# One layer of hybrid attention: a half's second x group is split in the middle of the second projection tile, and in the output stages both loads stand at the beginning

## The chip, the core and the metric

The kernel runs on one core of a Trainium2 chip. The metric is the device time of one launch in microseconds (us); lower is better. The core has five engines that work through their own instruction streams, each in order: TensorE (PE in the rows, with PEld for its weight loads), VectorE (DVE), ScalarE (ACT), GpSimd (POOL) and SyncE (SP), which issues all of this kernel's transfers.

## What is computed

One decoder layer over 2048 tokens of width 1024. RMSNorm, one combined input projection, two attention mixers with eight heads each, gates, one output projection and the residual:

```python
hdn = rmsnorm(x, norm_gain[i])
proj = jnp.einsum("bsd,de->bse", hdn, w_in[i])
q_a, k_a, v_a, g_a, q_b, k_b, v_b, g_b = jnp.split(proj, split_at, axis=-1)
...
o_a, _, _ = banded_attention(q_a, k_a, v_a, A_WINDOW - 1, sinks=sinks_a[i])
o_a = o_a.reshape(b, S, A_WIDTH).astype(x.dtype) * jax.nn.silu(g_a)
...
o_b = dilated_attention(q_b, k_b, v_b)
o_b = o_b.reshape(b, S, B_WIDTH).astype(x.dtype) * jax.nn.silu(g_b)
mixed = jnp.concatenate([o_a, o_b], axis=-1)
x = x + jnp.einsum("bse,ed->bsd", mixed, w_out[i])
```

Mixer A is a causal window of 128 tokens with learned sinks. Mixer B attends under three patterns (window, dilation) and merges them by their softmax denominators. All of it is float32.

## The kernel before, in words

**Stages, blocks, halves.** Eight stages run one after the other: four of kind B (two heads of mixer B each), two of kind A (four heads of mixer A each), two of kind O (512 output columns each). A stage goes over four blocks of 512 tokens, and a block over two halves of 256 tokens; that makes 64 halves. In a B or A stage a half has two projection tiles (`tt` 0 and 1, 128 tokens each, eight chunks `c` of the 1024 input columns) and then one (B) or two (A) gate tiles of eight chunks. In an O stage a half has two output tiles.

**x in two parts.** A float32 product is made of three matmuls over a high and a low part of each operand (`mm3`, L244 in the rows). So a half needs its x, or in the O stages its mixed input, as xh and xl. `x_load` brings half of it (512 KB, four chunks, tile `xs`, two buffers); a half has two such loads, 0 and 1. `x_split` makes two chunks of it: a copy on ScalarE to xh (L155) and a subtraction to xl (L157), on GpSimd for groups 0 and 1 and for the last two halves of a stage, on VectorE otherwise. A half has four such groups; 0 and 1 read load 0, 2 and 3 read load 1. xh and xl have six buffers each, so group 2 of the next half takes the buffer of this half's group 0. In the first stage ScalarE also squares the next half's x (`squares`, L189), VectorE and a matmul with a column of ones sum it up (L198), and GpSimd raises it to a power: rst, the row factor of the norm (L182). rst is then transposed on TensorE (L211) into RB.

**Leaving PSUM.** When a projection tile is done, ScalarE squares its q and k part (sq, L409) and copies its v part with rst as scale (V, L410); VectorE then makes the rotary products (L419, L421) and the rest of V (L310). With that the tile's PSUM buffer (pj, two of them) is free for the tile after next.

**What sets the order.** `proj` is a generator that yields after every chunk; between the yields a driver puts in the pieces of attention that are due (scores, transposes, products with V, merging). The order so written is not yet the program's: the framework's scheduler takes the instructions of all engines with their dependencies and its own estimate of their times, and lays down each engine's stream. It can put an instruction far ahead of its place in the code when its inputs and buffers are free. Each engine, and the SP queue, then keeps to that stream.

The places that the change touches are in `proj` (B and A stages) and `proj_out` (O stages), where the next half `nx` is prepared. At the program's beginning `late_constants` also fills the zero rows of two tiles klz on GpSimd (L90).

Of the kernel before, what the change touches and what calls it, by code (L numbers as in the profile page):

```python
# [28 lines left out]
def f32(ap):  # L29
    return ap.bitcast(F32)  # L30
# [3 lines left out]
def hybrid_layer(ctx, tc, xT, xn, x, wB, wA, wO, ng, gains, sinks, rot, masks, ident, out):  # L34
# [116 lines left out]
    def x_split(si, hf, g):  # L151
        f = XS[si, hf, g // 2][:, 2 * (g % 2):2 * (g % 2) + 2]
        h = xp.tile([128, 2, 256], F32R, name="xh", bufs=XB)
        l = xp.tile([128, 2, 256], F32R, name="xl", bufs=XB)
        nc.scalar.activation(h, f, AF.Copy)  # L155
        eng = nc.gpsimd if g < 2 or hf >= 6 else nc.vector
        eng.tensor_tensor(l, f, f32(h), op=OP.subtract)  # L157
        XG[si, hf, g] = (h, l)
# [87 lines left out]
    def proj(si, sb):  # L246
# [22 lines left out]
        for half in range(2):  # L269
            hf = 2 * sb + half  # L270
            nx = next_half(si, hf)
# [6 lines left out]
            for tt in range(2):  # L278
# [3 lines left out]
                for c in range(KC):  # L282
                    xh, xl = xg[c // 2]
                    s = slice(tt * 128, tt * 128 + 128)
                    mm3(pj, (xh[:, c % 2, s], xl[:, c % 2, s]), wq[c], c, c == 0, c == KC - 1)
                    if last and half == 1 and tt == 1:
                        W[si + 1][2](c)
                    yield 490
                if tt == 0 and nx:
                    x_load(*nx, 1)  # L290
                    x_split(*nx, 0)
                    x_split(*nx, 1)
                    if si == hf == 0:
                        late_constants(1)
                        rb_make(0)
                    rope_tables(*nx)
                    if si == 0 and hf < 7:
                        for g in range(2):
                            squares(XS[nx + (g,)], g)
                    rb_load(*nx)  # L300
# [214 lines left out]
    def proj_out(si, sb, wq, wg, last):  # L515
# [4 lines left out]
        for half in range(2):  # L520
            hf = 2 * sb + half
            nx = next_half(si, hf)
            xg = [XG.pop((si, hf, g)) for g in range(4)]
            if nx:
                x_load(*nx, 0)
            for tt in range(2):
                r = 2 * half + tt
                orow = bass.AP(tensor=out.tensor, offset=out.offset + (512 * sb + r) * DM + idx * 512, ap=[[4 * DM, 128], [1, 512]])
# [4 lines left out]
                for n in range(2 * KC):  # L533
# [7 lines left out]
                    if last and half == 1 and tt == 1:  # L541
                        W[si + 1][2](c)
                        W[si + 1][3](c)
                    if nx and tt == 1 and c in (1, 3):
                        x_split(*nx, 2 + c // 2)
                    yield 650
                while deferred:
                    yield from deferred.pop(0)()
                if tt == 0 and nx:
                    x_load(*nx, 1)  # L550
                    x_split(*nx, 0)
                    x_split(*nx, 1)
                res_load()
                if tail:
                    for o in range(2):
# [484 lines left out]
```

## Time and profile before

| | us |
|---|---|
| three runs | 1264.9, 1262.76, 1270.4 (median 1264.9) |
| the profiled execution | 1271.72 |
| its span, first to last instruction | 1269.9 |
| TensorE busy | 1179.8 (93%) |
| VectorE, ScalarE, GpSimd busy | 867.5, 837.1, 685.3 |
| mean granted TensorE clock | 0.970 of 2.4 GHz |

In the rows further down each instruction is named by line, engine, operation and out<-in tiles, without buffer numbers; "[2.27 <-POOL xl L157]" says that its engine stood idle for 2.27 us before it and what ended that. A matmul's length in the rows covers its pipeline, so neighbours overlap. The granted clock is 1.0 or 0.5, which is 2.4 or 1.2 GHz.

### The profile page before, as it was taken

Reading aid. Unit: us, or ns where it says so; the run is one execution under the profiler, and the core shown is the slowest. Engines: PE = TensorE matmul, PEld = TensorE weight load, DVE = VectorE, ACT = ScalarE, POOL = GpSimd, SP = SyncE. Lnnn points to the kernel's source line nnn. Section 1 sums busy time; section 2 is a strip of 40 time slices with the busy share of each in tenths; the row PEclk is TensorE's granted clock in tenths of the full one; section 3 lists DMA queues with packets and bytes.
Section 4 is the critical chain, followed back from the end, with each engine's and each line's share of the span. In section 5 each row is a group of like instructions: output and inputs, shape, how many; then the busy total and the mean of one; then the engine's idle time right before and its main releaser. Section 6 shows DMA issues by size and latency. Waiting matters only on the chain. (4 is left out here: it accounts for less than half of the span.)

```text
span 1269.9 us, 25442 instructions
## 1 busy us (share of the span) xinstructions
PE 1179.8 (93%) x8328; PEld 1143.5 (90%) x8328; DVE 867.5 (68%) x2288; ACT 837.1 (66%) x2418; POOL 685.3 (54%) x788
## 2 busy tenths in 40 slices
PE   6898979988799898898998999999899999999899
PEld 6798979988699898898997999998799998999898
DVE  5666678776667677776877879888777868622221
ACT  6567777777668587676877767786776877513221
POOL 4876644566454755545676566673556565333122
PEclk9899989999999899898998999999899999999999
DMA  7454678776677776787866775555223235566551
GB/s 215 128 148 114 176 214 243 211 202 185 193 212 232 198 198 181 219 235 197 221 200 191 212 199 150 149 165 165 91 73 109 80 97 157 164 197 205 177 188 70
DMA packets 196883, 220.98 MB, mean 174 GB/s; under 512 B 34312, under 2 KB 143632, under 8 KB 196752
## 3 DMA queue, kind: packets, MB, share of 16 engines
q1 hardware_dynamic: 196752, 219.37, 59.2%
q8 instruction: 66, 1.08, 0.4%
q14 instruction: 65, 0.53, 0.1%
HBM read 164.44 MB, written 54.86 MB: 173 GB/s over the span
## 5 line engine op out<-in xcount | busy, mean ns | idle before, releaser
L244 PE MATMUL pj<-wh,xh 128*128 128x384 f32 (+1 forms) x1008 | 334.1, 334 | 18.6 <-ACT xh L155 6.7
L244 PE MATMUL pj<-wl,xh 128*128 128x384 f32 (+1 forms) x1008 | 334.9, 332 | 1.4 <-DVE wl L102 0.8
L244 PE MATMUL pj<-wh,xl 128*128 128x384 f32 (+1 forms) x1008 | 331.9, 331 | 1.1 <-POOL xl L157 0.8
L157 POOL TENSOR_TENSOR xl<-xs,xh 128x512 fp32r<-128x512 f32 x158 | 213.7, 1365 | 143.8 <-ACT xh L155 139.1
L155 ACT ACTIVATE xh<-xs 128x512 fp32r<-128x512 f32 x252 | 153.5, 627 | 115.8 <-PE pj L244 98.8
L244 PEld LDWEIGHTS pj<-wh,xh 128*128 128x128 f32 x1008 | 194.4, 193 | 22.4 <-ACT xh L155 7.1
L244 PEld LDWEIGHTS pj<-wl,xh 128*128 128x128 f32 x1008 | 194.6, 193 | 3.6 <-DVE wl L102 1.1
L244 PEld LDWEIGHTS pj<-wh,xl 128*128 128x128 f32 x1008 | 194.4, 193 | 3.5 <-DVE xl L157 1.3
L574 DVE TENSOR_TENSOR ptl<-pt,pth 128x512 fp32r<-128x512 f32 (+3 forms) x232 | 141.6, 619 | 42.2 <-ACT pth L573 40.2
L244 PE MATMUL pj<-xh,wgh 128*128 128x256 f32 x496 | 147.1, 297 | 10.7 <-DVE V L310 8.4
L244 PE MATMUL pj<-xh,wgl 128*128 128x256 f32 x496 | 145.3, 293 | 0.0
L244 PE MATMUL pj<-xl,wgh 128*128 128x256 f32 x496 | 144.7, 292 | 0.0
L573 ACT ACTIVATE pth<-pt 128x512 fp32r<-128x512 f32 (+3 forms) x232 | 123.1, 543 | 25.6 <-PE po L645 9.4
L430 POOL TENSOR_TENSOR t<-t,t 128x256 f32<-128x256 f32 (+1 forms) x96 | 79.2, 826 | 80.9 <-DVE t L421 57.2
L244 PEld LDWEIGHTS pj<-xh,wgh 128*128 128x128 f32 x496 | 97.7, 197 | 12.9 <-DVE V L310 5.8
L446 DVE TENSOR_TENSOR t<-t,fac 128x256 f32<-128x256 f32 (+1 forms) x96 | 76.9, 815 | 33.0 <-POOL fac L182 30.1
L244 PEld LDWEIGHTS pj<-xh,wgl 128*128 128x128 f32 x496 | 97.7, 197 | 0.8
L814 ACT ACTIVATE P<-P,scD 128x128 f32<-128x128 f32 (+3 forms) x128 | 71.6, 560 | 40.5 <-DVE scD L813 39.6
L244 PEld LDWEIGHTS pj<-xl,wgh 128*128 128x128 f32 x496 | 97.8, 197 | 0.4
L157 DVE TENSOR_TENSOR xl<-xs,xh 128x512 fp32r<-128x512 f32 x94 | 79.8, 859 | 20.2 <-ACT xh L155 19.8
L182 POOL TENSOR_TENSOR fac<-un,mhalf 128x8 f32<-128x8 f32 (+1 forms) x48 | 85.3, 1778 | 2.7
L599 ACT ACTIVATE P<-P,scA 128x256 f32<-128x256 f32 (+1 forms) x128 | 63.1, 495 | 23.4 <-DVE scA L598 23.0
(188 smaller groups left out, 3087.8 us busy)
## 6 DMA issues: line engine op xcount, KB each, us to landing
xs<-in_xT SPq DMA_DIRECT2D x94, 512.0 KB
xs<-mx SPq DMA_DIRECT2D x32, 512.0 KB
vd<-V SPq DMA_DIRECT2D x64, 128.0 KB
qd<-qc SPq DMA_DIRECT2D x32, 256.0 KB
TT<-tab SPq DMA_DIRECT2D x32, 256.0 KB
cv<-vd SPq DMA_DIRECT2D x32, 256.0 KB
cq<-qd SPq DMA_DIRECT2D x32, 256.0 KB
ck<-kd SPq DMA_DIRECT2D x64, 128.0 KB
```

The costliest lines, as they stand in the source:

```text
L155: nc.scalar.activation(h, f, AF.Copy)
L157: eng.tensor_tensor(l, f, f32(h), op=OP.subtract)
L182: nc.gpsimd.tensor_tensor(y, u, mhalf.to_broadcast([128, n]), op=OP.pow)
L244: nc.tensor.matmul(o, a, b, start=first and n == 0, stop=last and n == 2, skip_group_check=True)
L430: nc.gpsimd.tensor_tensor(t1[:, :n], t1[:, :n], t2[:, :n], op=OP.add)
L446: nc.vector.tensor_tensor(t1v, t1v, fac[:, tt, :, None].to_broadcast([128, nh, 64]), op=OP.mult)
L573: nc.scalar.activation(hi, pt, AF.Copy)
L574: nc.vector.tensor_tensor(lo, pt, f32(hi), op=OP.subtract)
L599: nc.scalar.activation(pd, pd, AF.Exp, bias=nb[i], scale=-1.0, accum_out=l[i])
L814: nc.scalar.activation(pd, pd, AF.Exp, bias=nb, scale=-1.0, accum_out=l)
```

## The change

In a B or A stage group 1 of the next half is no longer split right after group 0, at the end of tile 0, but in tile 1, after chunk 3. In an O stage both loads of the next half are called at the half's beginning, group 0 is still split after tile 0, and groups 1, 2 and 3 are split in tile 1, after chunks 1, 3 and 5.

```diff
@@ proj (stages B and A)
                     if last and half == 1 and tt == 1:
                         W[si + 1][2](c)
+                    if nx and tt == 1 and c == 3:
+                        x_split(*nx, 1)
                     yield 490
                 if tt == 0 and nx:
                     x_load(*nx, 1)
                     x_split(*nx, 0)
-                    x_split(*nx, 1)
@@ proj_out (stages O)
             if nx:
                 x_load(*nx, 0)
+                x_load(*nx, 1)
...
-                    if nx and tt == 1 and c in (1, 3):
-                        x_split(*nx, 2 + c // 2)
+                    if nx and tt == 1 and c in (1, 3, 5):
+                        x_split(*nx, 1 + c // 2)
                     yield 650
...
                 if tt == 0 and nx:
-                    x_load(*nx, 1)
                     x_split(*nx, 0)
-                    x_split(*nx, 1)
```

The scheduler then lays down other streams. Three places, each before and then after; numbers behind names count tiles, and line numbers past L290 are one higher after the change.

GpSimd near the program's beginning (`xl` of x tile 258 are groups 0 and 1 of the second half), before:

```order
L157 TENSOR_TENSOR xl_289<-xs_258,xh_288 128x512
L90 TENSOR_SCALAR klz0_89<-mk_77 64x640 x2
L90 TENSOR_SCALAR klz1_90<-mk_77 64x640
L157 TENSOR_TENSOR xl_293<-xs_258,xh_292 128x512
L90 TENSOR_SCALAR klz1_90<-mk_77 64x640
L182 TENSOR_TENSOR rst_83<-rss_204,mhalf_85 128x2
```

and after:

```order
L157 TENSOR_TENSOR xl_289<-xs_258,xh_288 128x512
L90 TENSOR_SCALAR klz0_89<-mk_77 64x640 x2
L90 TENSOR_SCALAR klz1_90<-mk_77 64x640 x2
L182 TENSOR_TENSOR rst_83<-rss_204,mhalf_85 128x2
L157 TENSOR_TENSOR xl_365<-xs_258,xh_364 128x512
```

Group 1's subtraction (xl_293, now xl_365) moved behind the fourth fill and behind rst.

ScalarE a little later (xs_459 and xs_487 are the two loads of the third half, xs_659 the first of the fourth; V_336 or V_332 and V_389 leave the first two projection tiles), before:

```order
L155 ACTIVATE xh_489<-xs_459 128x512
L155 ACTIVATE xh_493<-xs_459 128x512
L189 ACTIVATE cq_505<-xs_459 128x512
L189 ACTIVATE ck_506<-xs_459 128x512
L189 ACTIVATE cq_512<-xs_487 128x512
L189 ACTIVATE ck_513<-xs_487 128x512
L155 ACTIVATE xh_607<-xs_487 128x512
L410 ACTIVATE V_336<-pj_261,rst_83 128x2x64
L410 ACTIVATE V_389<-pj_355,rst_83 128x2x64
```

and after:

```order
L155 ACTIVATE xh_489<-xs_459 128x512
L189 ACTIVATE cq_501<-xs_459 128x512
L189 ACTIVATE ck_502<-xs_459 128x512
L155 ACTIVATE xh_539<-xs_459 128x512
L411 ACTIVATE V_332<-pj_261,rst_83 128x2x64
L411 ACTIVATE V_389<-pj_351,rst_83 128x2x64
L213 ACTIVATE RB_308<-po_305 128x256
L335 ACTIVATE gz_438<-G_257 128x256
L189 ACTIVATE cq_508<-xs_487 128x512
L189 ACTIVATE ck_509<-xs_487 128x512
L155 ACTIVATE xh_607<-xs_487 128x512
```

The two copies V, with RB and the gate's tanh (gz), moved ahead of the squares of load xs_487; group 1's copy (xh_493, now xh_539) moved behind the squares of its own load.

ScalarE in the second stage, around a gate tile (xs_2865 is the second load of one half, xs_3143 the first of the half after it), before:

```order
L155 ACTIVATE xh_3066<-xs_2865 128x512
L476 ACTIVATE Q_2141<-po_2940 128x2x128
L477 ACTIVATE KK_2143<-po_2940 128x8x32
L155 ACTIVATE xh_3099<-xs_2865 128x512
L814 ACTIVATE P_3011,scD_2844<-P_3011,scD_2844 128x256
L155 ACTIVATE xh_3234<-xs_3143 128x512
L573 ACTIVATE pth_87<-pt_3002 128x384
L155 ACTIVATE xh_3238<-xs_3143 128x512
```

and after:

```order
L155 ACTIVATE xh_3066<-xs_2865 128x512
L814 ACTIVATE P_3011,scD_2844<-P_3011,scD_2844 128x384
L155 ACTIVATE xh_3099<-xs_2865 128x512
L155 ACTIVATE xh_3234<-xs_3143 128x512
L573 ACTIVATE pth_87<-pt_3002 128x384
L814 ACTIVATE P_3011,scD_2844<-P_3011,scD_2844 128x256
L155 ACTIVATE xh_3267<-xs_3143 128x512
```

The four copies stand in the same sequence in both, groups 2 and 3 of one half and 0 and 1 of the next; the rows between them moved.

## Rows read from the trace of the kernel before

**Rows 1.** The page, part 1: engine, busy us, share, instructions.

```profile
PE 1179.8 (93%) x8328; PEld 1143.5 (90%) x8328; DVE 867.5 (68%) x2288; ACT 837.1 (66%) x2418; POOL 685.3 (54%) x788
```

**Rows 2.** Four B, one O stage: length, busy PE, PEld, DVE, ACT, POOL, clock, DMA, GB/s.

```profile
5.56:156.69 151.13, 134.34 (x858) 129.87 (x858) 103.50 (x242) 102.52 (x279) 105.81 (x141) 0.93 0.53 155
156.69:325.95 169.26, 151.55 (x1043) 147.30 (x1042) 121.06 (x330) 123.57 (x361) 90.17 (x112) 0.98 0.74 209
325.95:500.56 174.61, 160.41 (x1070) 154.38 (x1071) 125.15 (x340) 127.17 (x373) 96.17 (x117) 0.95 0.73 205
500.56:672.35 171.79, 162.10 (x1089) 157.00 (x1089) 129.34 (x350) 129.74 (x380) 97.87 (x119) 0.95 0.74 211
...
1058.37:1167.34 108.97, 107.09 (x888) 106.10 (x886) 49.37 (x106) 46.54 (x115) 38.31 (x31) 1.00 0.59 184
```

**Rows 3.** List of waits, TensorE: total us, times, longest.

```profile
PE pj L244 <- DVE V L310: 11.9, 9, 4.3
```

**Rows 4.** Timeline of ScalarE, second stage: start, us, what, idle before.

```profile
219.54 0.62 ACT L155 ACTIVATE xh<-xs 128x512 fp32r<-128x512 f32 x1
...
222.50 0.65 ACT L155 ACTIVATE xh<-xs 128x512 fp32r<-128x512 f32 x1
...
225.26 0.42 ACT L334 ACTIVATE gz<-G 128x256 f32<-128x256 f32 x1
```

**Rows 5.** Timeline of ScalarE, first output stage.

```profile
1140.11 0.63 ACT L155 ACTIVATE xh<-xs 128x512 fp32r<-128x512 f32 x1 [6.62 <-PE pj L244]
```

**Rows 6.** Timeline of GpSimd, 22 to 37 us.

```profile
23.04 6.18 POOL L90 TENSOR_SCALAR klz<-mk 64x640 fp32r<-64x640 f32 x3
29.30 1.26 POOL L157 TENSOR_TENSOR xl<-xs,xh 128x512 fp32r<-128x512 f32 x1
30.53 1.81 POOL L90 TENSOR_SCALAR klz<-mk 64x640 fp32r<-64x640 f32 x1
32.31 0.72 POOL L182 TENSOR_TENSOR rst<-rss,mhalf 128x2 f32<-128x2 f32 x1
```

**Rows 7.** Timeline of TensorE, 20 to 60 us.

```profile
30.61 0.44 PE L244 MATMUL sc<-wh,xl 128*128 128x384 f32 x1 [2.27 <-POOL xl L157]
...
35.62 0.95 PE L198 MATMUL po<-one,o1c 128*128 128x1 f32 x8
...
46.88 0.44 PE L244 MATMUL pj<-wh,xh 128*128 128x384 f32 x1 [2.57 <-ACT xh L155]
...
58.05 0.69 PE L211 MATMUL po<-idf,rst 128*128 128x128 f32 x2 [2.86 <-POOL rst L182]
```

**Rows 8.** Windows, same columns, by granted clock.

```profile
26.70:47.20 20.50, 15.40 (x102) 14.55 (x101) 11.43 (x24) 7.66 (x18) 16.31 (x17) 1.00 0.42 128
47.20:50.60 3.40, 3.09 (x10) 2.65 (x9) 2.65 (x8) 2.46 (x8) 3.40 (x8) 0.50 0.39 130
57.40:67.70 10.30, 9.42 (x41) 9.13 (x42) 6.34 (x20) 7.48 (x21) 9.86 (x17) 0.50 0.35 105
```

**Rows 9.** Timeline of ScalarE, first stage.

```profile
34.40 0.63 ACT L189 ACTIVATE cq<-xs 128x512 f32<-128x512 f32 x1 [1.90 <-DMA xs<-in_xT]
...
35.98 0.61 ACT L410 ACTIVATE V<-pj,rst 128x128 fp32r<-128x128 f32 x2
...
44.89 0.63 ACT L189 ACTIVATE cq<-xs 128x512 f32<-128x512 f32 x1 [3.95 <-DMA xs<-in_xT]
...
46.21 0.62 ACT L155 ACTIVATE xh<-xs 128x512 fp32r<-128x512 f32 x1
...
112.17 0.63 ACT L189 ACTIVATE cq<-xs 128x512 f32<-128x512 f32 x1 [1.89 <-DMA xs<-in_xT]
```

**Rows 10.** Timeline of the SP queue, 26 to 50 us.

```profile
30.59 0.33 SPq L148 DMA_DIRECT2D xs<-in_xT  x1
38.97 0.65 SPq L314 DMA_DIRECT2D vd<-V  x1
39.74 0.36 SPq L148 DMA_DIRECT2D xs<-in_xT  x1
```

## The prediction

> **What bounds the kernel now.** I read the page's busy times first, then the stretches stage by stage, then the list of waits, then the timelines of the places where TensorE stood still. TensorE is busy 93% of the span [rows 1], and the reader should see that the missing 7% lies in the first two thirds. In the first B stage it is busy 134.3 of 151.1 us at a mean granted clock of 0.93, in the third 160.4 of 174.6 at 0.95, in the first output stage 107.1 of 109.0 at 1.00 [rows 2]. So TensorE sets the time, and an edit is worth what it takes from, or adds to, TensorE's holes, plus what the clock loses after them: after the hole that ends at 46.88 the granted clock is 0.50 for 3.4 us, after the one that ends at 58.05 it is 0.50 up to 67.7, though it was 1.00 from 26.7 to 47.2 [rows 7, 8]. At 0.50 (the lower level, 1.2 GHz) half of such a stretch is lost: 1.7 us of 3.4.
>
> **The output stages: nothing.** The edit issues both loads of a half at its start and puts the splits one to every second chunk. But the program's order is made by a scheduler, and it had hoisted all of this already: in the order printed for both kernels the last 133 instructions of ScalarE, 152 of the SP queue and 2041 of TensorE read the same, and that covers both output stages whole. The trace shows why nothing was to be had: before a split in the middle of the first output stage ScalarE stands idle for 6.62 us until a matmul frees the buffer, not until a transfer lands [rows 5], and TensorE loses 1.9 us in this stage [rows 2]. I cost these two edits at 0. Their cover is the wait for the buffers; were it gone, a late load would cost about what the stage loses now, 1.9 us.
>
> **The B and A stages, from the second half on: no move of the split itself.** The edit calls the split of group 1 half a tile of the projection later, 12 of its 24 matmuls. In the steady order, however, the two first splits of a half run nearly a whole half earlier than their place in the code: in the trace four copies stand in a row, 219.54 to 222.50, ahead of the gate's tanh at 225.26 [rows 4], and the order names them as groups 2 and 3 of one half and 0 and 1 of the next. In the changed kernel's order the same four stand in the same place (the third piece of order above). So of the 48 splits of group 1 that the edit moves in the B and A stages all but the first few (a copy of 0.63 us and a subtraction of some 1.3 us each) keep their cover, and the edit costs 0 there. What does change is the order of the rows around them: the priorities differ, and from the first half until late in the second A stage many rows have other neighbours. I call this the reshuffle. Its sign can't be read off; its size can be bounded by the trace: the second, third and fourth B stage do the same kind and amount of work in three different orders, and took 169.3, 174.6 and 171.8 us [rows 2], a standard deviation of 2.7 us. Five stages are affected beside the first, at most; 2.7 x the square root of 5 is 6.0 us. I take 0 for it and keep plus or minus 7.7 (1.28 times 6.0) for the range.
>
> **The first B stage: a loss, then a gain.** Here the scheduler has nothing to hoist from, so the edit bites.
>
> Loss, at 28.3 us. TensorE waits 2.27 us, until 30.61, for group 1's subtraction on GpSimd [rows 7], which stands behind three of the four fills of the zero tiles (6.18 us together) and runs at 29.30 in 1.26 us [rows 6]. In the changed order it stands behind all four and behind the power for rst. From the same start: 23.04 + 6.18 + 1.9 (the fourth fill, 1.81 when alone) is 31.1, plus 0.72 for rst is 31.8, plus 1.26 is 33.1. TensorE resumes 2.5 us later. It now has the transposes and column sums for rst (L211, L198) ahead of this matmul, some 1.2 us that it did later before (35.40 to 36.57, of which the second row shows 0.95) [rows 7], so 1.3 us net. A hole of nearly 5 us may also bring the clock down, where the 2.27 us left it at 1.00 [rows 8]. The nearest row is the hole of 2.57 us that was followed by 3.4 us at 0.50; I take one and a half such stretches, 2.6 us. Bounds: 0 and 5.2 (the 10.3 us stretch). Loss: 1.3 + 2.6 = 3.9.
>
> The Trainium skill says in TensorE: Matmul & The Clock Gate, "What's actually happening", that the throttled clock is the default and that activity releases it. [...]
>
> Gain, at 44.3 and 55.2 us. Before, the two copies that evict the projection (V, L410) stood behind the squares of the next half's second load; these waited for their transfer until 34.40, so V ran at 35.98 [rows 9], though rst was ready at 33.0 (0.72 after 32.31 [rows 6]). SP is in order: the store of V was issued at 38.97 and the following load of x behind it at 39.74 [rows 10]. That load is what the squares at 44.89 wait 3.95 us for, and the copy that TensorE wants, xh of group 3, runs behind them at 46.21 [rows 9]: the hole of 2.57 us [rows 7]. In the changed order V stands ahead of those squares, right behind rst: some 2 us sooner after rst, so the store and with it the load that matters go out at about 36 to 37 instead of 39.74. (The load ahead, for groups 2 and 3 of this half, moves behind the store: about 35 instead of 30.59 [rows 10]. With 3.8 us to its squares, as in the trace (34.40), it is there at 39, while the half that needs it begins at 42 to 43. That slack of 3 to 4 us covers it.) Then the copy of group 3 runs near 45, when TensorE wants it near 46: the hole goes, 2.57 us and 1.7 of clock. The next one, 2.86 us for rst at 58.05 [rows 7], falls for the same reason: on GpSimd this power then stands ahead of one subtraction of x and of the norm's power, and its inputs come earlier. 2.9 us, and of the 10.3 us of low clock behind it I count one stretch of 3.4 us, 1.7, since other holes lie in that region. Gain: 2.6 + 1.7 + 2.9 + 1.7 = 8.9. Bounds: 0, if another wait takes its place, and 12.3 with the whole low stretch.
>
> **Sum.** 3.9 - 8.9 = -5.0 us against the profiled execution's 1271.7 us (span 1269.9 and 1.8 around it), so 1266.7. That execution is 0.5% above the median of 1264.9; 5.0/1271.7 of the median leaves 1260 us.
>
> **Rivals.** (a) The change does nothing: the row order is different but each hole comes back at a like place, such as those at a stage's beginning, where the weights' transfers come late, which the edit does not touch. 1265 us. For it speaks that the splits keep their places in nearly all halves. (b) The longer chain on GpSimd decides, slower: subtraction at 33.1, the clock down for 10.3 us as behind 58.05 (5.2), and everything behind it (the second rst, the next splits) late by the same, so that no gain follows: 1.3 + 5.2 = 6.5, 1271 us. It decides when the second rst on GpSimd, some 42 us by the chain, is later than TensorE's arrival there, which I also put near 42; that is close. (c) The reshuffle is bad: V behind squares that wait for a load, as at 112.17 [rows 9], where the wait for V cost 4.3 us [rows 3] and the clock 1.7, comes twice more: 1265 + 12 = 1277. (d) The reshuffle is good: two such holes vanish beside the gain: 1260 - 12 = 1248. Against (c) and (d) speaks the small spread of three B stages; for them, that in a deterministic order a hole once there stays.
>
> **How the numbers follow.** Forecast 0.42, (a) 0.20, (b) 0.15, (c) 0.10, (d) 0.13. The likeliest gives 1260. Around each case I set a spread of 8.4 us: the reshuffle's 6.0, 5 for the first stage's terms (between their bounds) and 3 for the runs' own spread (1262.8 to 1270.4), added as squares; so the forecast by itself gives 1249 to 1271 (1.28 x 8.4) in 8 of 10. For 8 in 10 over all cases I reach into (c) and (d): 1243 to 1276. One per cent is 12.6 us, and about what a measurement of this kernel tells from no change. Below 1252.3 lie seven tenths of (d), a fifth of the forecast and a tenth of (a), 0.09 + 0.08 + 0.02 = 0.19; above 1277.5 half of (c), a fifth of (b) and little of the others, 0.05 + 0.03 + 0.02 = 0.10. The spread is from three stages only, so I put 0.03 and 0.02 more into the tails: 0.22 and 0.12, and 0.66 within 1%.
>
> **What would show it.** In the changed profile: TensorE's wait for xl near 28 us grows to some 5 us; the waits for xh near 45 and for rst near 56 are gone, and the clock is at 1.00 near 48; the first B stage is 144 to 149 us long instead of 151; the output stages are within 1 us of 109.0 and 102.6. Wrong would be: a first B stage of 155 us or more (b), or B and A stages that move by more than 8 us in sum, one way or the other (c, d), or a changed output stage, against the identical order.

## The result and the profile after

The changed kernel takes 1259.8 us in the median of nine runs (1257.4 to 1263.7) against 1267.5 us of the kernel before in as many (1262.8 to 1276.0): a ratio of 0.9934, 95% interval 0.9908 to 0.9960. It is faster, by less than one per cent: 7.7 us by the medians, 8.4 by the ratio. Its profiled execution has a span of 1259.4 us against 1269.9.

The busy times hardly moved, by the first part of the page of the changed kernel:

```profile
PE 1174.8 (93%) x8328; PEld 1141.3 (91%) x8328; DVE 850.7 (68%) x2288; ACT 834.7 (66%) x2418; POOL 680.4 (54%) x788
```

TensorE is busy 1174.8 us where it was 1179.8 [rows 1], with the same 8328 matmuls. What moved shows stage by stage. These are the windows of the changed kernel from each stage's first matmul to the next one's, in the columns of [rows 2]:

```profile
5.50:150.87 145.37, 130.53 (x855) 126.88 (x855) 102.54 (x242) 101.92 (x279) 106.43 (x141) 0.95 0.56 162
150.87:314.35 163.48, 153.75 (x1057) 149.82 (x1056) 120.41 (x338) 124.56 (x364) 87.73 (x110) 0.97 0.77 217
314.35:487.35 173.00, 158.51 (x1064) 153.85 (x1065) 123.66 (x338) 127.20 (x368) 98.63 (x118) 0.94 0.72 206
487.35:661.11 173.76, 159.08 (x1076) 153.42 (x1075) 125.64 (x342) 128.39 (x376) 96.82 (x119) 0.95 0.74 209
661.11:866.15 205.04, 194.22 (x1373) 187.56 (x1371) 162.21 (x471) 150.69 (x458) 126.32 (x142) 0.98 0.58 172
866.15:1045.37 179.22, 174.31 (x1259) 168.44 (x1260) 143.74 (x417) 131.89 (x421) 102.77 (x105) 1.00 0.32 101
1045.37:1156.30 110.93, 108.53 (x887) 107.54 (x886) 48.40 (x106) 47.14 (x116) 38.29 (x32) 0.98 0.59 184
1156.30:1259.40 103.10, 95.83 (x770) 93.82 (x768) 23.66 (x38) 20.57 (x37) 23.08 (x18) 0.98 0.46 150
```

The first B stage takes 145.4 us instead of 151.1, the second 163.5 instead of 169.3 [rows 2]. The two A stages must be read together, since the first now holds 1373 matmuls in place of 1349 and the second 1259 in place of 1274. These are their windows in the kernel before, which add up to 386.0 us; the changed kernel's add up to 384.3.

```profile
672.35:871.43 199.08, 190.15 (x1349) 183.72 (x1350) 167.67 (x461) 147.12 (x446) 129.18 (x143) 0.98 0.61 176
871.43:1058.37 186.94, 179.62 (x1274) 172.47 (x1273) 147.21 (x426) 137.28 (x431) 104.11 (x105) 0.98 0.32 99
```

The first output stage takes 110.9 instead of 109.0 [rows 2].

Since one execution differs from the next, every statement on stages below rests on this table of profiled executions, one line each, all from such windows (us; the order of a program is what the scheduler lays down for each engine). The runs are those of the next section; the four lines called third differ from one another in some 3 of 100 rows of ScalarE.

| kernel | order behind the first stage | first B | B 2 to 4 | both A | both O |
|---|---|---|---|---|---|
| before | before | 151.1 | 515.7 | 386.0 | 211.6 |
| output edit alone | before | 149.6 | 515.0 | 381.5 | 212.5 |
| all but the first half | nearly before | 149.5 | 516.6 | 385.1 | 211.3 |
| before, test appended at the end | before | 147.5 | 510.8 | 383.8 | first O 109.0 |
| changed | changed | 145.4 | 510.2 | 384.3 | 214.0 |
| B and A edit alone | changed | 142.5 | 509.6 | 383.3 | 211.3 |
| first half alone | nearly changed | 145.0 | 512.8 | 381.0 | 214.2 |
| changed, fills on VectorE | third | 138.6 | 510.9 | 383.4 | 212.7 |
| before, fills on VectorE | third | 138.2 | 509.5 | 382.0 | 212.7 |
| before, one subtraction on VectorE | third | 147.0 | 511.2 | 382.9 | 215.7 |
| changed, the same subtraction on VectorE | third | 146.2 | 510.4 | 382.9 | 211.8 |
| before, two small fills on VectorE | fourth | 146.0 | 505.1 | 384.7 | 212.0 |
| before, one negation on GpSimd | fifth | 146.2 | 511.1 | 382.1 | 212.9 |

The executions profiled lie up to 5 us off the medians of their kernels, so their stages are long or short by about that in sum: that of before 4.2 us above, those of the output edit alone and of the B and A edit alone 4.1 and 4.2 below, those with the fills on VectorE 5.2 and 4.5 below, that of the last line 4.5 below. A profile of that last kernel at a mean granted clock of 0.66 (1571.6 us), and two more executions as far off (1574.0 and 4100.8 us), are not used.

The fourth line is of the last run of the next section, a test that is appended behind the last residual sum. Up to there its TensorE, ScalarE and SP queue run in exactly the order of before, so it is a fourth profile of that order. From its second B stage to the beginning of its last output stage it takes 1003.6 us; the three lines above it take 1010.7, 1005.5 and 1010.7, and the three of the changed order 1005.4, 1002.6 and 1004.8.

### The profile page after: what moved, and what is told of

Its sections match the earlier page's. It is cut to its first block, busy times and chain, and to the rows that moved or that the text cites. A ratio compares the mean times of both kernels' runs of the same rounds, so it can differ in the third digit from the quotient of the medians.

```text
span 1259.4 us, 25438 instructions
## 1 busy us (share of the span) xinstructions
PE 1174.8 (93%) x8328; PEld 1141.3 (91%) x8328; DVE 850.7 (68%) x2288; ACT 834.7 (66%) x2418; POOL 680.4 (54%) x788
## 4 chain that ended last, share of the span: by engine, by line
PE 55%; DMA 16%; DVE 10%; ACT 8%; POOL 6%; issue 3%; SPq 2%; POOLq 0%; ACTq 0%; DVEq 0%
PE pj L244 39%; DMA xs<-in_xT 3%; DMA Rb<-rD 2%; DMA stg<-in_wB 2%; PE po L849 2%; DMA stg<-in_wO 2%; DMA stg<-in_wA 2%; PE sc L590 1%; PE sc L591 1%; PE po L645 1%; PE pt L828 1%; PE po L735 1%; PE pt L719 1%; ACT P L599 1%; DVE ptl L574 1%
## 5 line engine op out<-in xcount | busy, mean ns | idle before, releaser
L157 POOL TENSOR_TENSOR xl<-xs,xh 128x512 fp32r<-128x512 f32 x158 | 210.3, 1341 | 146.3 <-ACT xh L155 136.6
L244 PE MATMUL pj<-xl,wgh 128*128 128x256 f32 x496 | 145.4, 293 | 0.0
L814 ACT ACTIVATE P<-P,scD 128x256 f32<-128x256 f32 (+3 forms) x128 | 71.6, 560 | 33.6 <-DVE scD L813 32.9
L157 DVE TENSOR_TENSOR xl<-xs,xh 128x512 fp32r<-128x512 f32 x94 | 76.9, 823 | 21.1 <-ACT xh L155 20.5
L447 DVE TENSOR_TENSOR t<-t,fac 128x256 f32<-128x256 f32 (+1 forms) x96 | 67.4, 710 | 30.8 <-POOL fac L182 23.7
L813 DVE CUSTOM_DVE_ANT_0 P<-sc,mk 128x256 f32<-128x256 f32 (+3 forms) x128 | 61.1, 484 | 32.2 <-PE sc L809 31.5
```

What stands on the lines that cost most here:

```text
L244: nc.tensor.matmul(o, a, b, start=first and n == 0, stop=last and n == 2, skip_group_check=True)
L447: nc.vector.tensor_tensor(t1v, t1v, fac[:, tt, :, None].to_broadcast([128, nh, 64]), op=OP.mult)
L813: nc.vector.tensor_tensor_reduce(pd, o[:, :m], m2[:, 512 - m:], -0.125, BIG, OP.add, OP.min, nb)
L814: nc.scalar.activation(pd, pd, AF.Exp, bias=nb, scale=-1.0, accum_out=l)
```

## The experiments

**Which part of the edit acts.** Four runs take the change apart. The first has the edit of the B and A stages alone:

```diff
+                    if nx and tt == 1 and c == 3:
+                        x_split(*nx, 1)
                     yield 490
                 if tt == 0 and nx:
                     x_load(*nx, 1)
                     x_split(*nx, 0)
-                    x_split(*nx, 1)
```

> Only the edit of the B and A stages (the split of group 1 at c == 3 of the second projection tile); the output stages keep the code of before. Theory (the output edits are worth nothing): the printed order of this kernel reads like that of the changed kernel on every engine, so the time is that of the changed kernel, 0.993 of before (0.990 to 0.996), and the output stages take 110.9 and 103.1 us, each within 1.5 us. Rival (the output edits matter): output stages back at 109.0 and 102.6 us and a ratio that differs from 0.993 by more than 0.002. This run is also a second profile of the same order, so the stage lengths against those of the changed kernel show how far one execution differs from the next.

Measured: 1258.5 us, 0.9919 (0.9891 to 0.9947), output stages 109.6 and 101.7 us. The second has the edit of the output stages alone:

```diff
                 x_load(*nx, 0)
+                x_load(*nx, 1)
...
-                    if nx and tt == 1 and c in (1, 3):
-                        x_split(*nx, 2 + c // 2)
+                    if nx and tt == 1 and c in (1, 3, 5):
+                        x_split(*nx, 1 + c // 2)
...
-                    x_load(*nx, 1)
                     x_split(*nx, 0)
-                    x_split(*nx, 1)
```

> Only the edit of the output stages (both loads at the start, splits 1, 2, 3 at c = 1, 3, 5); the B and A stages keep the code of before. Theory: the printed order reads like that of before on every engine, ratio 1.000 (0.998 to 1.002). Rival (the loads at the start are worth something): ratio 0.997 or less, output stages shorter by 3 us in sum. As a second profile of the order of before it shows the spread of its stage lengths between executions; I expect the first B stage at 151.1 within 2 us and the other stages within 4 us each.

Measured: 1269.8 us, 1.0017 (0.9997 to 1.0036). So the output edits are worth nothing that these runs can tell, as both theories' numbers asked. The two runs are second profiles of the two orders as well: stage by stage they lie within 3 us of the first ones. The run with the appended test, in the order of before, lies up to 3.6 us off.

The third and the fourth put the moved split into the very first half alone, and into all halves but that one:

```diff
+                    if nx and tt == 1 and c == 3 and (si == hf == 0):
+                        x_split(*nx, 1)
...
-                    x_split(*nx, 1)
+                    if not (si == hf == 0):
+                        x_split(*nx, 1)
```

> The split of group 1 is moved in the very first half of the program alone; all 47 others stay where before has them. Its printed order follows that of the changed kernel nearly everywhere: on ScalarE 3 to 10 of 100 rows differ from it, where 40 to 80 of 100 differ from before. Theory (the first half makes all of it, the direct gain in the first stage and the reshuffle behind it): 0.993 of before (0.990 to 0.996), first B stage 145 us. Rival (the 47 later splits carry a part): between 0.996 and 1.000, with a first stage of 145 us and later stages like those of before.

```diff
+                    if nx and tt == 1 and c == 3 and (not (si == hf == 0)):
+                        x_split(*nx, 1)
...
-                    x_split(*nx, 1)
+                    if not (not (si == hf == 0)):
+                        x_split(*nx, 1)
```

> The reverse: the split of group 1 is moved in every half of the B and A stages but the very first. Its order follows that of before (3 to 6 of 100 rows of ScalarE differ). Theory (the later moves cost nothing): 1.000 of before (0.997 to 1.003), first B stage 151 us. Rival (the later moves carry the gain): 0.996 or less, with a first B stage of 151 us; or they cost something, 1.003 or more.

Measured: 0.9925 (0.9901 to 0.9949) for the first half alone, 1.0003 (0.9978 to 1.0028) for the 47 others. The whole gain comes from one moved call out of 48, and the 47 others cost and bring nothing that shows. That call does two things. It changes the first stage, by 5.8 us (150.1 us in the mean of the first three lines of the table, 144.3 in that of the three lines of the changed order), or by 5.1 with the fourth profile of before's order (149.4). And since the scheduler lays down everything behind it anew, it changes the order of the later stages: from the second B stage to the end 1106.9 us instead of 1111.7, the means of the same three lines each. This second part is not clear of the spread: up to the beginning of the last output stage the difference is 4.7 us by three profiles of before's order and 3.3 by four, and those four lie 7 us apart among themselves. That the whole gain of 8 is more than the 5 to 6 of the first stage speaks for it.

In the first stage the gain is TensorE's holes and the clock, in like parts. In the kernel before TensorE has no matmul in 16.8 of its 151.1 us [rows 2], and the granted clock is 0.50 for 20.5 us; without the holes and half of that, 124.1 us are left. In the changed kernel it is 14.8 of 145.4 us, with 13.7 us at 0.50, and 123.7 are left. In all seven profiles of the two orders it is 122.4 to 124.1. Over the four profiles of the one order and the three of the other the holes fall from 15.1 to 12.6 us in the mean, and the time at 0.50 from 22.2 to 17.1, half of which counts.

**What the new order does later.** Holes are bound to an order. These waits of TensorE stand at the end of the second B stage of the kernel before:

```profile
297.83 0.53 PE L474 MATMUL po<-idr,hl 128*128 128x128 f32 x4 [1.68 <-POOL hl L457]
...
305.84 0.52 PE L835 MATMUL pt<-idf,P 128*128 128x128 f32 x3 [1.51 <-DVE ptl L574]
...
325.95 0.41 PE L244 MATMUL pj<-wh,xh 128*128 128x384 f32 x1 [4.14 <-ACT xh L155]
```

and these in the run with the output edit alone, which has the same order:

```profile
298.18 0.54 PE L474 MATMUL po<-idr,hl 128*128 128x128 f32 x4 [2.45 <-POOL hl L457]
306.18 0.52 PE L834 MATMUL pt<-idf,P 128*128 128x128 f32 x3 [1.51 <-DVE ptl L573]
325.04 0.66 PE L244 MATMUL pj<-wh,xh 128*128 128x384 f32 x1 [2.86 <-ACT xh L155]
```

The same three waits for the same tiles, of 1.5 to 4.1 us. The other two profiles of this order have them at the same places, of 1.1 to 3.3 us; in one of them the last of the three ends with V on VectorE. In the three profiles of the changed order no wait above 1 us stands between 255 us and the end of that stage; its large ones are elsewhere (in the changed kernel 4.6 us near 325 for KK, 5.0 near 430 for ptl, 5.7 near 672 for V).

**Whether another order is better by chance.** The two last orders of the table come from edits that move no split: one instruction of 0.2 us, or two of 0.5 us, on another engine.

```diff
-        nc.vector.tensor_scalar(nsk, sk, -1.0, None, op0=OP.mult)
+        nc.gpsimd.tensor_scalar(nsk, sk, -1.0, None, op0=OP.mult)
```

> The kernel before with one instruction of 0.2 us (the negation of the sinks, a 128x8 tile) on GpSimd instead of VectorE; no split is moved. In its order rows have other neighbours from the first half until the end of the first A stage (30 to 90 of 100 rows of ScalarE), and from the second A stage on it reads like before. The three orders so far took, from the second B stage to the end, 1111.7 us (before, mean of three profiles), 1106.9 (changed, three) and 1106.5 (the four runs with fills or a subtraction on VectorE). Theory (the order behind the first stage is a draw of holes, and that of before is no special one): anything from 1104 to 1115, with the second A stage at 185 as before and holes at other places than before. Rival (the order of before is a bad one, and whatever disturbs it is 4 to 5 us better): 1108 or less, the second to fourth B stage at 511 or less in sum (515.7 before).

> The kernel of the run with the negation of the sinks on GpSimd once more, for a profile at the usual clock (the first one was taken at a granted clock of 0.66 on average, so its stages can't be set beside the others). It was 0.9965 of before, 4.4 us faster. Theory (a draw of holes behind an untouched first stage): first B stage at 149 to 151 us, second A stage at 185, the second to fourth B stage together 509 to 515 (515.7 before), with the waits near 296, 304 and 322 us of before gone or at other places. Rival (the first stage is what got shorter): first B stage 147 or less, the rest at 1111.7 within 2.

Measured: 0.9965 (0.9938 to 0.9991), and in the second run 0.9970 (0.9937 to 1.0004), which does not exclude 1. The first B stage came out at 146.2, not at the 149 to 151 I expected, though its waits near 45 and 55 us for xh and rst are there (2.23 and 3.07 us): the large wait near 111 us shrank to 1.4. With before's own order at 147.5 in one profile, and this execution 4.5 us below its median, that is no clear change. The rest is as the theory put it (511.1 and, for the second A stage, 186.5), and the rival's 1111.7 for all behind the first stage is not met (1106.2).

```diff
-            nc.gpsimd.tensor_scalar(t[:, 5, :], idf, 0.0, None, op0=OP.mult)
+            nc.vector.tensor_scalar(t[:, 5, :], idf, 0.0, None, op0=OP.mult)
```

> The kernel before with two small fills of 128x128 (0.5 us each, of the constants) on VectorE instead of GpSimd; no split is moved. Another order behind the first half, which differs from all the others and ends from the second A stage on like the changed kernel. Theory (a draw of holes): second B stage to the end 1104 to 1115 us, the second A stage at 178 as in the changed order. Rival (any other order is better than that of before): 1108 or less.

Measured: 1255.3 us, 0.9880 (0.9837 to 0.9923), with 1101.9 us from the second B stage to the end. That is below the range of the theory (1104 to 1115), and it meets the rival's. So edits that have nothing to do with x move this kernel by some 4 and by 15 us. All four orders other than that of before are faster than it. If the five were draws alike, the one of before would still be the slowest of them once in five times, so this does not make it a special one; whether it is, and why, stays open.

**What acts in the first stage.** Two runs move the four fills of klz to VectorE, in the changed kernel and in the one before:

```diff
-                nc.gpsimd.tensor_scalar(zt, mk[z, 0:640], 0.0, None, op0=OP.mult)
+                nc.vector.tensor_scalar(zt, mk[z, 0:640], 0.0, None, op0=OP.mult)
```

> The changed kernel with the four fills of the zero tiles (klz, L90) on VectorE instead of GpSimd. In its order GpSimd runs both subtractions, rst and the first TT products without a fill ahead of them, and on ScalarE the two V copies stand ahead of all squares of the next half. Theory (the fills ahead of rst and of the subtraction make the loss): TensorE's wait for rst near 27 us (4.29 us in the changed kernel) and the low clock behind it are gone, first B stage 136 to 141 us (144.3 is the mean of three profiles of the changed order). The later stages fall into a third order; I expect them in sum (second B to last) at 1109 us, plus or minus 6 (1111.7 in the order of before, 1106.9 in the changed one, means of three). Ratio to before 0.988, plus or minus 0.005. Rival (TensorE waits at this place for the transfer of x anyway): first stage 143 us or more.

> The kernel before with the four fills on VectorE, the split of group 1 where before has it. The V copies come out ahead of the squares here too, and from the second B stage on the order is that of the run with the same edit on the changed kernel but for a few swapped neighbours. Theory (the place of V and the fills decide, the place of the split does not): first B stage within 3 us of that run, 136 to 142 us against 150.1 of before; later stages in sum within 5 us of it. Rival (the moved split itself brings the gain): first stage 144 us or more.

Measured: 0.9911 (0.9887 to 0.9935) and 0.9893 (0.9863 to 0.9923), the first stage 138.6 and 138.2 us, in executions 5.2 and 4.5 us below their medians. By GpSimd's timeline in the run on the changed kernel nothing stands ahead of the subtractions and rst any more:

```profile
21.37 3.68 POOL L157 TENSOR_TENSOR xl<-xs,xh 128x512 fp32r<-128x512 f32 x2
25.01 1.00 POOL L182 TENSOR_TENSOR rst<-rss,mhalf 128x2 f32<-128x2 f32 x1
```

rst is there at 26.0 instead of 31.5, and TensorE has no wait above 1.1 us between 23 and 50 us. VectorE fills faster, all four in 3.05 us against 7.95 (its timeline in the same run):

```profile
20.18 3.05 DVE L90 TENSOR_SCALAR klz<-mk 64x640 fp32r<-64x640 f32 x4
```

The place of the split is worth nothing here: 0.4 us between the two. That the wait for rst goes with the fills is shown; whether these versions beat the changed kernel as a whole the intervals don't tell.

The next pair puts the subtraction of group 1 for the second half on VectorE, in the kernel before and in the changed one:

```diff
-        eng = nc.gpsimd if g < 2 or hf >= 6 else nc.vector
+        eng = nc.gpsimd if (g < 2 and (si, hf, g) != (0, 1, 1)) or hf >= 6 else nc.vector
```

> The kernel before with one instruction on another engine: the subtraction of group 1 for the second half (the one behind three fills) runs on VectorE. In its order it runs before the fills and TensorE has no wait for it; but all four fills stand ahead of rst, and the V copies stand behind four squares, of two loads, instead of two. Theory (the place of V decides): the wait of 2.27 us at 28 us is gone, but the holes near 44 and 55 us come back or grow: first B stage 149 to 156 us. Rival (the wait for the subtraction was what mattered in the first stage): 144 to 148 us. Later stages: the third order again.

> The changed kernel with the same instruction on VectorE. Its split is moved as in the changed kernel, but its order has the V copies behind four squares. Theory (the moved split gains only by letting V pass the squares): the gain of the first stage is lost, 149 to 156 us, within 3 us of the run before with the same edit. Rival (the moved split gains by itself): 145 us or less.

Measured: 0.9935 (0.9910 to 0.9961) and 0.9942 (0.9922 to 0.9963), first stage 147.0 and 146.2. Again the place of the split makes no difference, and the rival's 145 or less for the second run is not met either. But the theory that the place of V decides fell: it asked for 149 to 156. ScalarE runs V behind four squares, later than before (35.98 [rows 9]), by the timeline of the first of the two runs:

```profile
36.77 0.61 ACT L410 ACTIVATE V<-pj,rst 128x128 fp32r<-128x128 f32 x2
```

and no wait for xh or rst stands near 44 or 55 us (others do, 1.97 us near 48 for RB and 3.43 near 58 for P, and the granted clock is 0.50 from 50.0 to 67.1). In that order the load of x is issued ahead of the store of V (37.82 and 38.75), so a late V keeps nothing back. In these runs, then, a late V cost TensorE a wait where a load stood behind its store, and none where the load stood ahead of it.

**A disputed wait.** In two of the three profiles of the changed order VectorE's sum of squares takes over four times as long as in the third. VectorE's timeline in the changed kernel:

```profile
31.80 3.73 DVE L190 TENSOR_TENSOR cq<-cq,ck 128x512 f32<-128x512 f32 x1 [4.52 <-ACT ck L189]
```

the same row in the run with the B and A edit alone:

```profile
31.93 0.85 DVE L190 TENSOR_TENSOR cq<-cq,ck 128x512 f32<-128x512 f32 x1 [4.39 <-ACT ck L189]
```

and in the run with the first half alone:

```profile
31.62 3.93 DVE L190 TENSOR_TENSOR cq<-cq,ck 128x512 f32<-128x512 f32 x1 [4.67 <-ACT ck L189]
```

In the first and the third GpSimd had begun a subtraction just before (31.51 and 31.52), in the second it began after (32.12). But there another instruction of VectorE with two inputs, 0.41 us in the changed kernel, began just behind the first of two subtractions on GpSimd (34.86 to 37.36) and ended 0.3 us after the second. VectorE's timeline in the run with the B and A edit alone:

```profile
34.95 2.70 DVE L191 TENSOR_TENSOR o1c<-cq 128x256 f32<-128x256 f32 x1
```

A test behind the last residual sum, where all other engines are done, measured this by itself:

```diff
+        for first, op1, second, op2 in ((P, add, V_, add), (V_, add, P, add), (P, add, V_, one), (P, one, V_, add)):
+            for rep in range(2):
+                add(first, a, xr, xr)
+                add(first, b, a, a)
+                if op2 is add:
+                    add(second, c, a, xr)
...
+                for n in range(5):
+                    if op1 is add:
+                        add(first, d, xr, xr)
...
+                add(first, a, c, d)
+                add(second, xr, a, b)
```

> The kernel before with a test appended behind the last residual sum, where no other engine works: one engine runs additions of 128x512 back to back, and behind the first of them, while the next ones run, the other engine starts one operation. Four cases, each twice: GpSimd adds, VectorE adds; VectorE adds, GpSimd adds; GpSimd adds, VectorE scales (one input); GpSimd scales (one input), VectorE adds. It settles what made VectorE's sum of squares take 3.73 and 3.93 us in two profiles of the changed order and 0.85 in the third. Theory (an addition with two inputs from SBUF waits while the other engine holds the way to SBUF, longer than one operation): in the first case VectorE's addition takes 2 to 6 us instead of 0.69, in the third case the scaling takes 0.4 to 0.7. Rival (it waited for something else, its inputs or an evicted tile): below 1 us in all cases.

On GpSimd, in the first case (its second repetition) and in the fourth:

```profile
1268.85 2.04 POOL L572 TENSOR_TENSOR xs<-cq 128x512 f32<-128x512 f32 x2 [0.81 <-DVE cq L572]
1270.85 1.49 POOL L572 TENSOR_TENSOR xs<-xs 128x512 f32<-128x512 f32 x1
...
1315.08 1.50 POOL L575 TENSOR_SCALAR xs<-cq 128x512 f32<-128x512 f32 x1
```

and on VectorE, an addition alone, the one of the first case, and the ones of the third and fourth:

```profile
1268.08 0.69 DVE L572 TENSOR_TENSOR cq<-xs 128x512 f32<-128x512 f32 x1 [6.62 <-POOL xs L572]
1269.93 1.51 DVE L572 TENSOR_TENSOR xs<-xs,cq 128x512 f32<-128x512 f32 x1 [1.15 <-POOL xs L572]
...
1295.73 1.25 DVE L575 TENSOR_SCALAR xs<-xs 128x512 f32<-128x512 f32 x1 [2.49 <-POOL xs L572]
...
1315.15 1.09 DVE L572 TENSOR_TENSOR xs<-xs,cq 128x512 f32<-128x512 f32 x1 [1.15 <-POOL xs L572]
```

The addition takes 1.51 us instead of 0.69: it begins 1.0 us before GpSimd's running addition ends (1270.89) and gets done 0.55 us after that, while GpSimd's next one is stretched to 1.49. So there is such a wait, but it is of one instruction, below the 2 to 6 us of the theory, and scaling with one input waits too (1.25, where the theory had 0.4 to 0.7). The rival's 1 us or less is not met in these three cases either. In the second case, where VectorE adds first, GpSimd's addition takes 1.58 us and VectorE's next one 1.75. The rule of the Trainium skill (SBUF — State Buffer, "Who interferes with whom"), that of these two engines the one that starts first keeps the shared way to SBUF for its whole instruction and the other waits until it ends, agrees with the first case. In the fourth VectorE's addition ends at 1316.24, before GpSimd's scaling does (1316.58), which that rule does not give. Nor does it reach 3.73 us, in which GpSimd ended five instructions. What else held VectorE there is open.

## Why the prediction came out as it did

The time came out where it was put, 1259.8 against 1260, and the first part of the argument is borne out: TensorE's holes and the clock behind them set the time, and the first stage changes by what they say. That it hit to 0.2 us is luck. The gain was sized too small (5 us; measured 7.7 by the medians, 8.4 by the ratio), and the median of three runs that it was taken from lay about as much too low (1264.9; nine runs give 1267.5). Some 3 to 5 us of the gain seem to come from a place that was costed at 0.

**The output stages, 0.** Right: the edit alone gives 1.0017. The first of them is 1.9 us longer all the same, against "within 1 us of 109.0", and so one of the prediction's own signs of being wrong. The order is the same, the arrival is not: ScalarE waits for the stage's weights in the changed kernel

```profile
1046.31 0.42 ACT L101 ACTIVATE wh<-stg 128x256 fp32r<-128x256 f32 x1 [1.63 <-DMA stg<-in_wO]
```

where it had no wait before. The copies to hl stand behind it and begin 2.1 us after the stage's first matmul instead of 0.7, and GpSimd's subtraction waits for them. Its result is what the transposes of hl read; the profile puts the end of TensorE's wait down to a copy of x that ends with this subtraction, near 1049.0. GpSimd and then TensorE, by the timelines of the changed kernel:

```profile
1047.96 1.07 POOL L458 TENSOR_TENSOR hl<-t,hl 128x256 fp32r<-128x256 f32 x1 [3.66 <-ACT hl L456]
```

```profile
1049.09 0.54 PE L485 MATMUL po<-idr,hl 128*128 128x128 f32 x4 [1.59 <-ACT xh L155]
```

An identical order was read as identical times; it isn't, where what comes in from ahead has shifted. Why the weights come late there the runs don't tell.

**The B and A stages from the second half on, no move.** Right for the splits: 47 moved calls cost 0.0003, well within the noise. The reshuffle was taken as 0 with plus or minus 7.7. For the five stages it is some -6 us by the means of three profiles each (-4.8 with the output stages) and -4.9 with the fourth profile of before's order: inside its range, and not clear of the spread between profiles. Two things in this step were off. The standard deviation of 2.7 us was that of one stage in one order; a change is the difference of two, so 2.7 times 1.4, 3.8 us a stage. Measured, the five stages moved by -4.5, -0.9, +0.6, +5.4 and -6.7 in the means. And the reshuffle was laid to 48 moved calls; it hangs on the first one.

**The loss at 28 us.** A hole of nearly 5 us and a stretch of low clock were forecast, 3.9 us net of both. GpSimd's timeline in the changed kernel has the four fills, then rst, then the subtraction, as the order said:

```profile
22.89 7.95 POOL L90 TENSOR_SCALAR klz<-mk 64x640 fp32r<-64x640 f32 x4
30.81 0.72 POOL L182 TENSOR_TENSOR rst<-rss,mhalf 128x2 f32<-128x2 f32 x1
31.51 1.26 POOL L157 TENSOR_TENSOR xl<-xs,xh 128x512 fp32r<-128x512 f32 x1
```

The sum put the subtraction's end at 33.1, measured 32.8. TensorE's timeline in the changed kernel:

```profile
31.58 0.69 PE L211 MATMUL po<-idf,rst 128*128 128x128 f32 x2 [4.29 <-POOL rst L182]
...
45.93 0.83 PE L198 MATMUL po<-one,o1c 128*128 128x1 f32 x6 [3.13 <-DVE o1c L191]
...
56.29 0.38 PE L211 MATMUL po<-idf,rst 128*128 128x128 f32 x2
```

The wait is 4.29 us (2.21 and 4.65 in the other two profiles of this order), and it is for rst, whose transposes stand ahead of the subtraction's matmul; with the 2.21 and 2.27 us of before gone and 1.56 and 4.29 in their place, TensorE stands 1.4 us longer, where 1.3 was worked out. The clock fell for 6.8 us, 3.4 lost instead of 2.6; a stretch of 3.4 us that before had from 23.3 on, not thought of, is gone in return (windows of the changed kernel by granted clock, columns as in [rows 8]):

```profile
30.00:36.80 6.80, 5.22 (x20) 5.22 (x21) 5.00 (x6) 2.97 (x7) 6.80 (x9) 0.50 0.08 27
...
47.10:50.50 3.40, 3.40 (x14) 3.40 (x13) 2.83 (x9) 3.10 (x9) 3.40 (x8) 0.50 0.03 4
57.40:67.70 10.30, 8.84 (x66) 8.29 (x66) 8.65 (x23) 9.39 (x27) 8.96 (x16) 1.00 0.36 110
```

So the loss is 1.4 + 3.4 - 1.7 = 3.1 us where 3.9 was forecast. With the fills on VectorE in the changed kernel both the wait and the low clock behind it are gone, so the fills make this loss. The first stage is 5.7 us shorter there (144.3 to 138.6), in an execution 5.2 us below its median.

**The gain at 44 and 55 us.** The hole near 55 for rst is gone in all three profiles of the changed order (56.29 above has no wait). In the changed kernel's profile the whole 10.3 us of low clock behind it is gone too, 5.2 us where 1.7 was counted; in the other two 3.4 us of it are left. Of the two reasons given, one holds: GpSimd runs this rst ahead of the norm's power and of one subtraction. Its input does not come earlier (VectorE is done with rss at 50.97 before and at 51.03 after). GpSimd's timeline in the kernel before, and then in the changed one:

```profile
57.11 0.89 POOL L182 TENSOR_TENSOR rst<-rss,mhalf 128x2 f32<-128x2 f32 x1
```

```profile
53.42 0.70 POOL L182 TENSOR_TENSOR rst<-rss,mhalf 128x2 f32<-128x2 f32 x1
```

The hole near 44 is the step that failed. V runs where it was put, at 32.20, right behind rst (ScalarE's timeline in the changed kernel):

```profile
32.20 0.60 ACT L411 ACTIVATE V<-pj,rst 128x128 fp32r<-128x128 f32 x2
42.22 0.63 ACT L189 ACTIVATE cq<-xs 128x512 f32<-128x512 f32 x1 [4.05 <-DMA xs<-in_xT]
```

But V has a second half on VectorE, and that stood behind the sum of squares of 3.73 us (VectorE's timeline in the changed kernel):

```profile
36.12 0.34 DVE L311 SCALAR_TENSOR_TENSOR V<-pj,rst,V 128x128 fp32r<-128x128 f32 x1
```

The working put this half's second load behind the store of V and yet at about 35, with the store at about 36: its order and its times did not agree. The SP queue of the changed kernel:

```profile
36.49 0.62 SPq L315 DMA_DIRECT2D vd<-V  x1
37.20 0.42 SPq L148 DMA_DIRECT2D xs<-in_xT  x1
...
38.98 0.65 SPq L148 DMA_DIRECT2D xs<-in_xT  x1
```

The store goes out at 36.49 as forecast, the load only behind it, at 37.20, and its squares start 5.0 us after that, not 3.8: the slack is used up, and TensorE waits 3.13 us for the column sums (o1c) in place of 2.57 for xh. Where the sum of squares took 0.85 us, the SP queue of the run with the B and A edit alone reads

```profile
33.74 0.62 SPq L315 DMA_DIRECT2D vd<-V  x1
34.46 0.42 SPq L148 DMA_DIRECT2D xs<-in_xT  x1
```

and no wait above 1 us stands near 44. Its first stage takes 142.5 us, 2.9 less than in the changed kernel's profile, though not for this alone: its wait for rst near 30 us is 2.1 us shorter too. So the chain from V's store over the load to TensorE is there as described, and the error is the time of the load at its head.

**The sum of the first stage.** Forecast -5.0, measured -5.1 to -5.8 by the means, and 145.4 us in the changed kernel's profile, inside the 144 to 149 named. It hits by errors that cancel: one hole less was saved than counted, and more of the low clock. By the terms above the changed kernel's profile gains 2.9 + 5.2 - 0.6 (3.13 for 2.57 near 44) - 3.1 = 4.4 us; the other 1.4 of its 5.8 come from smaller holes that the working did not name, such as the wait for V near 111 us (3.39 instead of 4.29).

**The rivals.** (a), holes come back at like places, describes the hole near 44 alone. (b), the chain on GpSimd decides and the time gets worse, fails: the subtraction was as late as it said, but the second rst, put at some 42, was done at 41.19, its transposes at 42.30 did not wait, and the gain behind 55 us came all the same. (c) and (d), a bad or good reshuffle of 12 us: neither in this size. With the two small fills on VectorE, 15 us faster in all, the stages behind the first were 9.8 us shorter than in the means of before's order, so a reshuffle near that size is possible.

## What to carry to other kernels

Where a scheduler decides the order, ask for each edit in which place of the program it can still act; here it was one call in 48, at the beginning, where the scheduler had nothing to hoist from. An edit there deals out the holes of the whole program anew, and edits with no other aim moved the time by 0.3 to 1.2 per cent here: a gain of that size is no proof that the edit's idea is right, and a change in it is sized as the difference of two draws. One profile of each order is not enough to see it: behind the first stage four of one order lay 7 us apart. Where an engine fills constants at the start, look at what stands behind the fills in its stream: on VectorE they took 3 us instead of 8 here, and the first stage lost its largest hole.

## What the hardware showed beyond that

The same hole need not have the same price. The working took from one execution that the hole of 2.27 us which ends at 30.61 leaves the clock at 1.00 [rows 7, 8]. The run with the output edit alone has the same order and the same hole:

```profile
30.54 0.44 PE L244 MATMUL sc<-wh,xl 128*128 128x384 f32 x1 [2.27 <-POOL xl L157]
```

Behind it the granted clock is 1.00 in the kernel before and 0.50 in this run, by a window of each:

```profile
30.70:34.10 3.40, 3.40 (x20) 3.40 (x21) 1.56 (x1) 1.81 (x4) 3.40 (x5) 1.00 0.50 160
```

```profile
31.00:34.40 3.40, 3.40 (x12) 3.40 (x12) 1.44 (x1) 1.61 (x4) 3.40 (x6) 0.50 0.45 154
```

The run with the B and A edit alone has the wait of 1.59 us at the start of the first output stage as the changed kernel has it:

```profile
1045.15 0.53 PE L485 MATMUL po<-idr,hl 128*128 128x128 f32 x4 [1.59 <-ACT xh L155]
```

Behind it the granted clock stays at 1.00, by this window of the same run:

```profile
1047.00:1053.00 6.00, 6.00 (x55) 6.00 (x54) 4.68 (x13) 5.05 (x20) 3.00 (x4) 1.00 0.94 277
```

while in the changed kernel it is at 0.50 for 3.4 us, the lower of the two levels (1.2 GHz):

```profile
1050.60:1054.00 3.40, 3.40 (x19) 3.40 (x18) 2.46 (x6) 2.08 (x8) 2.56 (x4) 0.50 0.92 275
```

The stage takes 109.6 us in the one and 110.9 in the other (111.0 in the run with the first half alone, where this hole was also followed by 3.4 us at 0.50). A price for the clock behind a hole, read from one execution, is thus no more than an estimate for the next.
